# A two-layer transformer trunk in split fp32: transposes of x moved ahead of a gain transpose, one scaling ahead of a weight cast, and the MLP norms' squares ten steps later

## The chip, the cores and the metric

The kernel runs on one core of a Trainium2 chip. The metric is the device time of one execution in microseconds (us); lower is better. Unless a sentence says otherwise, a time within an execution counts from the start of the profiled span.

## The reference

x is a block of 256 tokens by 2048 columns. Two layers follow one another: the first mixes the tokens by softmax attention with a forget gate (FoX, 16 heads of 128), the second by attention in three dilated windows. Each mixer has an RMS norm ahead of it and an MLP with an RMS norm behind it, and everything adds into x. All is fp32.

```python
def rms_norm(x, g):
    xf = x.astype(jnp.float32)
    y = xf * lax.rsqrt(jnp.mean(xf * xf, axis=-1, keepdims=True) + EPS)
    return (y * g.astype(jnp.float32)).astype(x.dtype)

def sq_relu_mlp(h, w_up, w_down):
    a = jax.nn.relu(h @ w_up)
    return (a * a) @ w_down
...
    for i in range(DEPTH):
        j = i // N_MIXERS
        h = rms_norm(x, mix_norm_g[i])
        ...
        x = x + mix.astype(x.dtype)
        h = rms_norm(x, mlp_norm_g[i])
        x = x + sq_relu_mlp(h, mlp_w_up[i], mlp_w_down[i]).astype(x.dtype)
```

## The kernel before

**Weights.** The products stream the weights: 539 MB go through the DMA queues in one execution. A weight *unit* is 256 rows by 512 columns. Its transfer fills a tile `raw` (ring of 5); ScalarE rounds it to `wh` (L398, a cast to the reduced format that TensorE multiplies at full rate); VectorE takes the remainder `wl = raw - wh` (L399); both lie in rings of 5. The left operand exists in two parts likewise, so a product is three matmuls: `wh` with the high part (L447), `wl` with the high part (L448), `wh` with the low part (L449). A unit feeds 12 matmuls of 128x512. In the trace a unit has its number in the names: `raw141`, `wh141`, `wl141`. In some parts of the MLP's up projection a scheme with fewer products of combined operands is used (the "wide" tiles, L1138 to L1140); for it VectorE also forms `sd` and `v` out of two raw tiles (L395 to L402) and sums of the left operand (`sums`, below).

**Norms.** `norm_chain` (L609) runs once for each column block n of x (four blocks `x0` to `x3` of 512 columns). A norm's scale for each token, `rstd`, is applied behind the product, so the left operand needs only x transposed and multiplied by the gain: `hT`, eight pieces pr = 0 to 7, high and low part. For the first norm (`n0`) TensorE transposes x (L626, tiles `ptx`), ScalarE scales the result into the high part (L628) and VectorE makes the low part (L629). For the two MLP norms, `n1` (layer 1) and `n3` (layer 2), x is transposed by VectorE and by transfers (`transposed_by_dma`, tile `turned`); ScalarE scales it into `room` (L552) and casts it to `hT` (L555), VectorE makes the low part (L557). Behind that, `token_sums` adds the rooms (L592 to L594, VectorE), ScalarE casts the sums (L606), VectorE takes their remainder (L609).

Last in each chain ScalarE squares the block and sums along the row: two instructions for a block, one for each 128 tokens (L638, out to a scratch tile `junk`). When all four blocks are done, VectorE makes the mean (L645, L646, tile `ms`), GpSimd raises it to the power -1/2 (L647) and VectorE squares that (L649, `rstd2`). For n1 and n3 `rstd2` is first used by `add_chain`, behind the first down projection.

**Order.** The program is written as generators that a small scheduler (`jobs`) advances by one step, a *tick*, for each six matmuls: `yield 2` means "go on two steps later", `yield ("n1", 3)` means "when that is done". What is issued in a tick goes behind what was issued before it in each engine's queue, and a later pass keeps that order. So `yield later` in `norm_chain`, just ahead of the squares, sets behind which casts the squares stand on ScalarE. The function `later` comes with the call of `normed`; where none is given, it is 2 steps.

**The opening.** x0 comes in three transfers (128, 128 and 256 columns), with the gain rows (`mix_rows`) between the first two; then come weights and x1, x2, x3 in turn. `gain_columns("g_mix", ...)` transposes the gain rows on TensorE (L194, `ps_g_mix`) and VectorE copies them to `gain` (L195); each scaling reads `gain`. The first two units are cast in two halves (`split_part`).

Of the kernel before, what the change touches and what calls it, by code (L numbers as in the profile page):

```python
# [9 lines left out]
F32 = mybir.dt.float32  # L10
# [7 lines left out]
P = 128  # L18
D = 2048
S = 256  # L20
# [3 lines left out]
KC = D // P  # L24
# [95 lines left out]
def trunk(ctx: ExitStack, tc, x, fox_w_in, fox_b_f, fox_q_gain, fox_k_gain, fox_w_out, dil_w_in,  # L120
          dil_q_gain, dil_k_gain, dil_w_out, mix_norm_g, mlp_norm_g, mlp_w_up, mlp_w_down, out):
    nc = tc.nc
# [40 lines left out]
    ident = const.tile([P, P], F32, name="ident")  # L163
# [17 lines left out]
    MLP_G, FOX_G, DIL_G = 2 * KC + 8, 2 * KC, 2 * KC + 2  # L181

    def gain_rows(name, sources):
        rows = work.tile([2 * KC + 8, P], F32, tag="s", name=name, bufs=S_BUFS)
        at = 0
        for src in sources:
            nc.sync.dma_start(rows[at:at + src.shape[0], :], src)
            at += src.shape[0]
        return rows[0:at, :]

    def gain_columns(name, rows, at):
        n = rows.shape[0]
        ps = ps_tp.tile([P, 512], F32, tag="tp", name=f"ps_{name}")
        nc.tensor.transpose(ps[:, :n], rows, ident[:n, :n])  # L194
        nc.vector.tensor_copy(gain[:, at:at + n], ps[:, :n])  # L195
# [4 lines left out]
    xt = [act.tile([P, NT, NC], F32, tag=f"x{n}", name=f"x{n}") for n in range(NX)]  # L200
# [176 lines left out]
    def split(parts=(slice(0, W_SUB),)):  # L377
        i = state["split"]
        if i >= len(units):
            return  # L380
        hi = wpool.tile([P, W_SUB, NC], F32R, tag="wh", name=f"wh{i}", bufs=W_BUFS)
        lo = wpool.tile([P, W_SUB, NC], F32R, tag="wl", name=f"wl{i}", bufs=W_BUFS)
        splits.append((hi, lo))
        state["split"] += 1
        for part in parts:
            split_part(i, part)
        if parts:
            next_load()

    def split_part(i, part):  # L390
        n, of = units[i]
        raw, (hi, lo) = raws[n], splits[i]
        if of == "crossed":
            quarters[:] = [work.tile([P, RAW_SUB, NC], F32, tag=x, name=f"{x}_{n}", bufs=1) for x in ("sd", "v")]
            nc.vector.tensor_sub(quarters[0], raw, raws[n - 1][:, 1, :].unsqueeze(1).to_broadcast([P, RAW_SUB, NC]))  # L395
        elif of != "rows":
            raw = quarters[("differences", "sums").index(of)]
        nc.scalar.copy(hi[:, part, :], raw[:, part, :])  # L398
        nc.vector.tensor_sub(lo[:, part, :], raw[:, part, :], hi[:, part, :].bitcast(F32))  # L399
        if of == "crossed":  # L400
            nc.vector.tensor_add(quarters[1][:, 0, :], raw[:, 0, :], quarters[0][:, 1, :])
            nc.vector.tensor_sub(quarters[1][:, 1, :], raws[n - 1][:, 0, :], quarters[1][:, 0, :])  # L402
# [3 lines left out]
    def next_load():  # L406


        n, of = units[state["split"] - 1]
        spent.update({"rows": (n,), "crossed": (n - 1, n)}.get(of, ()))  # L410
        while state["done"] in spent:
            state["done"] += 1
        while state["raw"] < min(len(plan), state["done"] + RAW_BUFS):
            load()
# [98 lines left out]
    def norm_begin(tag):  # L513
        rstd[tag] = small.tile([P, NT], F32, tag="rstd", name=f"rstd_{tag}", bufs=2)
        hT[tag] = [None] * (KC // 2)
        return small.tile([P, NT, NX], F32, tag="ssp", name=f"ssp_{tag}", bufs=2)
# [97 lines left out]
    def norm_chain(tag, col, n, ssp, wait, later):  # L614
        yield wait
        if tag != "n0":
            yield from transposed_by_dma(tag, col, n)
        else:
            for half in range(2):
                pr = n * 2 + half  # L620
                both = act.tile([P, 2, 2, S], F32R, tag="hT", name=f"hT_{tag}_{pr}", bufs=KC // 2)
                for i, (pool, of) in enumerate(((ps_tp, "tp"), (ps_sc, "sc"))):
                    pt = pool.tile([P, S], F32, tag=of, name=f"ptx_{tag}_{pr}_{i}")
                    c = (half * 2 + i) * P
                    for t in range(NT):
                        nc.tensor.transpose(pt[:, t * P:(t + 1) * P], xt[n][:, t, c:c + P], ident)  # L626
                    gc = gain[:, col + pr * 2 + i:col + pr * 2 + i + 1]
                    nc.scalar.activation(both[:, i, 0, :], pt, AF.Copy, scale=gc)  # L628
                    nc.vector.scalar_tensor_tensor(both[:, i, 1, :], pt, gc, both[:, i, 0, :].bitcast(F32),  # L629
                                                   ALU.mult, ALU.subtract)  # L630
                hT[tag][pr] = both
                jobs.done.add((tag, pr))
                yield 1 if n < 2 else 2
        yield later
        for t in range(NT):
            junk = work.tile([P, NC], F32, tag="vw" if tag in ("n0", "n2") else "w", name=f"junk_{tag}_{n}_{t}",
                             bufs=1 if tag in ("n0", "n2") else 6)
            nc.scalar.activation(junk, xt[n][:, t, :], AF.Square, accum_out=ssp[:, t, n:n + 1])  # L638
        jobs.done.add((tag, "n", n))
        if n == NX - 1:  # L640
            for m in range(NX):
                yield (tag, "n", m)
            ms = small.tile([P, NT], F32, tag="ms", name=f"ms_{tag}", bufs=2)
            rstd[tag, 2] = small.tile([P, NT], F32, tag="rstd2", name=f"rstd2_{tag}", bufs=2)
            nc.vector.tensor_reduce(ms, ssp, AX.X, ALU.add)  # L645
            nc.vector.tensor_scalar(ms, ms, 1.0 / D, EPS, ALU.mult, ALU.add)  # L646
            nc.gpsimd.tensor_tensor(rstd[tag], ms, mhalf[:, :NT], ALU.pow)  # L647
            yield 2 if tag in ("n1", "n3") else 0
            nc.vector.tensor_mul(rstd[tag, 2], rstd[tag], rstd[tag])  # L649
            jobs.done.add((tag, "rstd"))  # L650
# [547 lines left out]
    def normed(tag, col, wait=lambda n: 2, later=lambda n: 2):  # L1198
        ssp = norm_begin(tag)
        return lambda n: norm_chain(tag, col, n, ssp, wait(n), later(n))  # L1200
# [10 lines left out]
    def load_x(n, lo=0, hi=NC):  # L1211
        hold(xt[n])
        nc.sync.dma_start(xt[n][:, :, lo:hi], xv[:, :, n * NC + lo:n * NC + hi])

    load_x(0, 0, P)
    mix_rows = gain_rows("g_mix", [mix_norm_g.rearrange(per_chunk, p=P)])
# [7 lines left out]
    for what in (lambda: load_x(1), load, load, lambda: load_x(2), load):  # L1224
        what()

    gain_columns("g_mix", mix_rows, 0)
    row_blocks = [slice(i, i + 1) for i in range(W_SUB)]
    split(())
    split_part(0, row_blocks[0])  # L1230
# [1 line left out]
    split_part(0, row_blocks[1])  # L1232
    next_load()
    split(())
    split_part(1, row_blocks[0])
    load_x(3)
    del issued["paced"]
    issued["opening"] = True

    def opening():  # L1240
        yield 1
        split_part(1, row_blocks[1])
        next_load()
        yield 2
        split(row_blocks)
        yield 1
        split()
        for _ in range(5):
            yield 2
            split()  # L1250
        yield 1
        del issued["opening"]
        while state["split"] - used[0] < W_BUFS:
            yield 4
            split()

    for n in range(1, NX):
        jobs.spawn(first(n))
    jobs.spawn(opening())
    jobs.spawn(more_constants())  # L1260


    tag = "n0"
    for j in range(4):
# [10 lines left out]
        for hh in range(4):  # L1275
# [2 lines left out]

    out_proj(lambda n: lambda k: ("of", k),
             lambda k: (oT["f", k // 4][0][:, k % 4, :], oT["f", k // 4][1][:, k % 4, :]),  # L1280
             normed("n1", MLP_G), group=3)
    jobs.spawn(dilation_tables())
    mlp("n1", then=normed("n2", KC))
    dilated("n2")
    out_proj(lambda n: lambda k: ("od", k // 2),
             lambda k: (oT["d", k // 4][0][:, k % 4, :], oT["d", k // 4][1][:, k % 4, :]),
             normed("n3", MLP_G + KC), group=3)
    mlp("n3", ready=store)
    while jobs.live:
        jobs.tick()  # L1290
# [29 lines left out]
```

## Time and profile before

| | |
|---|---|
| median of 3 runs | 2084.84 us (2084.24 to 2085.33) |
| the profiled execution: its own time | 2084.9 us |
| the profiled execution: its span | 2083.2 us |
| busy: TensorE (PE), its weight loads (PEld) | 2076.8 us (100%), 1818.5 us (87%) |
| busy: VectorE (DVE), ScalarE (ACT), GpSimd (POOL) | 1714.9 us (82%), 1305.8 us (63%), 275.2 us (13%) |
| granted TensorE clock | 9 in tenths in all 40 slices of the span |
| DMA | mean 259 GB/s |

Rows of the timeline view read: start in us, duration in us, engine, line, operation, output tile <- input tiles, sizes, count; in brackets, where there is one, the idle time ahead of it and what ended it. Matmuls overlap: a 128x512 matmul has a record of 0.38 us, but the next one starts 0.215 us behind it. Tile numbers are left out of the names, so a weight unit is told by its place. A line number belongs to the kernel before; behind the changed lines those of the kernel after are three to four higher.

### The profile page before, as it was taken

What the parts mean: (1) busy time and instruction counts of PE and PEld (TensorE: products, weight loads), DVE (VectorE), ACT (ScalarE), POOL (GpSimd) and SP (SyncE); (2) the same over time, 40 slices, a digit from 0 to 9 for tenths busy, and PEclk for the clock granted to TensorE, in tenths of its full rate; (3) what the DMA queues carried; (4) which work ended last, traced back from release to release, by engine and by line L of the source; (5) the groups of instructions that cost most, each with busy time, mean ns of one, the idle gap of its engine ahead of it and who ended that gap; (6) DMA issues with size and microseconds to landing.
All of it is one profiled execution on the core that took longest, in us unless ns stands there. A gap on an engine that the chain in (4) does not pass through costs nothing.

```text
span 2083.2 us, 28968 instructions
## 1 busy us (share of the span) xinstructions
PE 2076.8 (100%) x9835; PEld 1818.5 (87%) x9835; DVE 1714.9 (82%) x2183; ACT 1305.8 (63%) x1825; POOL 275.2 (13%) x398
## 2 busy tenths in 40 slices
PE   9999999999999999999999999999999999999999
PEld 7888888888888888888888888888888888888888
DVE  6888876898989889888668787766998898899874
ACT  6665654866666667564656565556766676666662
POOL 2000000011212111120010010000113031212120
PEclk9999999999999999999999999999999999999999
DMA  7888887888988898897877876877889888898885
GB/s 254 259 259 260 262 248 212 267 285 262 268 281 269 262 296 269 267 291 247 279 242 229 250 239 210 260 212 237 262 272 272 278 276 265 276 287 276 265 280 165
DMA packets 357205, 539.04 MB, mean 259 GB/s; under 512 B 43752, under 2 KB 144448, under 8 KB 357056
## 3 DMA queue, kind: packets, MB, share of 16 engines
q1 hardware_dynamic: 334624, 507.41, 76.8%
q0 software_dynamic: 22016, 29.38, 6.2%
q8 instruction: 77, 1.26, 0.3%
q10 hardware_dynamic: 416, 0.39, 0.1%
q14 instruction: 72, 0.59, 0.1%
HBM read 484.09 MB, written 40.39 MB: 252 GB/s over the span
## 4 chain that ended last, share of the span: by engine, by line
PE 97%; ACT 1%; DMA 1%; DVE 1%; issue 0%; SPq 0%; ACTq 0%; DVEq 0%
PE acc L448 26%; PE acc L447 26%; PE acc L449 25%; PE wide_n_tp L1139 2%; PE wide_n_tp L1140 2%; PE wide_n_tp L1138 2%; PE wide_n_sc L1139 2%; PE wide_n_acc L1140 2%; PE wide_n_acc L1139 2%; PE wide_n_sc L1140 2%; PE wide_n_sc L1138 2%; PE wide_n_acc L1138 2%; PE sc_d L798 0%; DMA raw<-in_fox_w_in_dram 0%; ACT room_n L552 0%; ACT wh L398 0%
## 5 line engine op out<-in xcount | busy, mean ns | idle before, releaser
L399 DVE TENSOR_TENSOR wl<-raw,wh 128x1024 fp32r<-128x1024 f32 (+1 forms) x763 | 919.5, 1214 | 308.5 <-ACT wh L398 299.3
L398 ACT CAST wh<-raw 128x1024 fp32r<-128x1024 f32 (+1 forms) x763 | 787.2, 1046 | 505.5 <-PE acc L449 368.7
L447 PE MATMUL acc<-wh,hT_n 128*128 128x512 f32 x1280 | 486.7, 380 | 0.4 <-ACT hT_n L628 0.2
L448 PE MATMUL acc<-wl,hT_n 128*128 128x512 f32 x1280 | 485.6, 379 | 0.5 <-DVE wl L399 0.5
L449 PE MATMUL acc<-wh,hT_n 128*128 128x512 f32 x1280 | 485.4, 379 | 0.0
L449 PEld LDWEIGHTS acc<-wh,hT_n 128*128 128x128 f32 x1280 | 241.9, 189 | 34.8 <-DVE hT_n L629 0.4
L448 PEld LDWEIGHTS acc<-wl,hT_n 128*128 128x128 f32 x1280 | 242.1, 189 | 34.6 <-DVE wl L399 2.1
L447 PEld LDWEIGHTS acc<-wh,hT_n 128*128 128x128 f32 x1280 | 242.1, 189 | 34.3 <-ACT hT_n L628 1.2
L447 PE MATMUL acc<-wh,aTh_n1a 128*128 128x512 f32 x512 | 194.0, 379 | 0.0
L448 PE MATMUL acc<-wl,aTh_n1a 128*128 128x512 f32 x512 | 194.0, 379 | 0.0
L449 PE MATMUL acc<-wh,aTl_n1a 128*128 128x512 f32 x512 | 194.0, 379 | 0.0
L447 PE MATMUL acc<-wh,aTh_n3a 128*128 128x512 f32 x480 | 181.9, 379 | 0.0
L448 PE MATMUL acc<-wl,aTh_n3a 128*128 128x512 f32 x480 | 181.9, 379 | 0.0
L449 PE MATMUL acc<-wh,aTl_n3a 128*128 128x512 f32 x480 | 181.9, 379 | 0.0
L994 POOL DMA_DIRECT2D x<-y_n x96 | 84.7, 1331 | 479.9 <-ACT y_n L993 421.4
L398 ACT CAST wh<-sd 128x1024 fp32r<-128x1024 f32 x80 | 84.1, 1051 | 99.4 <-DVE sd L395 77.6
L398 ACT CAST wh<-v 128x1024 fp32r<-128x1024 f32 x80 | 84.1, 1051 | 54.3 <-PE acc L449 42.7
L448 PEld LDWEIGHTS acc<-wl,aTh_n1a 128*128 128x128 f32 x512 | 96.8, 189 | 13.8
L447 PEld LDWEIGHTS acc<-wh,aTh_n1a 128*128 128x128 f32 x512 | 96.8, 189 | 13.7
L449 PEld LDWEIGHTS acc<-wh,aTl_n1a 128*128 128x128 f32 x512 | 96.8, 189 | 13.7
L449 PEld LDWEIGHTS acc<-wh,aTl_n3a 128*128 128x128 f32 x480 | 90.7, 189 | 12.9
L447 PEld LDWEIGHTS acc<-wh,aTh_n3a 128*128 128x128 f32 x480 | 90.7, 189 | 12.9
(665 smaller groups left out, 3227.7 us busy)
## 6 DMA issues: line engine op xcount, KB each, us to landing
raw<-in_mlp_w_up_dram SPq DMA_DIRECT2D x296, 512.0 KB, 4.9
raw<-in_mlp_w_down_dram SPq DMA_DIRECT2D x256, 512.0 KB, 5.0
raw<-in_dil_w_in_dram SPq DMA_DIRECT2D x192, 256.0 KB, 3.6
raw<-in_fox_w_in_dram SPq DMA_DIRECT2D x94, 512.0 KB, 4.7
raw<-in_fox_w_out_dram SPq DMA_DIRECT2D x32, 512.0 KB, 4.9
raw<-in_dil_w_in_dram SPq DMA_DIRECT2D x32, 512.0 KB, 5.4
raw<-in_dil_w_out_dram SPq DMA_DIRECT2D x32, 512.0 KB, 4.4
x<-y_n POOLq DMA_DIRECT2D x96, 128.0 KB, 6.4
```

The lines of the kernel that those rows point to most:

```text
L398: nc.scalar.copy(hi[:, part, :], raw[:, part, :])
L399: nc.vector.tensor_sub(lo[:, part, :], raw[:, part, :], hi[:, part, :].bitcast(F32))
L447: nc.tensor.matmul(acc[t], ah[:, tok], hi, start=first, stop=False)
L448: nc.tensor.matmul(acc[t], ah[:, tok], lo, start=False, stop=False)
L449: nc.tensor.matmul(acc[t], al[:, tok], hi, start=False, stop=last)
L994: nc.gpsimd.dma_start(xt[n][:, t, h * HC:h * HC + HC], y, accum_op=ALU.add)
L1138: nc.tensor.matmul(banks[bank], ah, wh, start=what < 3 and of == 0, stop=False, **alone)
L1139: nc.tensor.matmul(banks[bank], ah, wl, start=False, stop=False, **alone)
L1140: nc.tensor.matmul(banks[bank], al, wh, start=False, stop=of == KC // 2 - 1, **alone)
```

## The change

Three edits. First, in the n0 chain both transposes of a piece stand ahead of its two scalings, and for the first piece the gain rows' transpose and copy stand between the transposes and the scalings, instead of ahead of everything. Second, the first half of unit 1 is cast one tick into `opening()`, instead of ahead of the tick loop. Third, the chains of n1 and n3 wait twelve ticks ahead of the squares instead of two.

```diff
--- before.py
+++ after.py
@@ -619,11 +619,15 @@
             for half in range(2):
                 pr = n * 2 + half
                 both = act.tile([P, 2, 2, S], F32R, tag="hT", name=f"hT_{tag}_{pr}", bufs=KC // 2)
+                turned = []
                 for i, (pool, of) in enumerate(((ps_tp, "tp"), (ps_sc, "sc"))):
-                    pt = pool.tile([P, S], F32, tag=of, name=f"ptx_{tag}_{pr}_{i}")
+                    turned.append(pool.tile([P, S], F32, tag=of, name=f"ptx_{tag}_{pr}_{i}"))
                     c = (half * 2 + i) * P
                     for t in range(NT):
-                        nc.tensor.transpose(pt[:, t * P:(t + 1) * P], xt[n][:, t, c:c + P], ident)
+                        nc.tensor.transpose(turned[i][:, t * P:(t + 1) * P], xt[n][:, t, c:c + P], ident)
+                if pr == 0:
+                    gain_columns("g_mix", mix_rows, 0)
+                for i, pt in enumerate(turned):
                     gc = gain[:, col + pr * 2 + i:col + pr * 2 + i + 1]
                     nc.scalar.activation(both[:, i, 0, :], pt, AF.Copy, scale=gc)
                     nc.vector.scalar_tensor_tensor(both[:, i, 1, :], pt, gc, both[:, i, 0, :].bitcast(F32),
@@ -1224,7 +1228,6 @@
     for what in (lambda: load_x(1), load, load, lambda: load_x(2), load):
         what()
 
-    gain_columns("g_mix", mix_rows, 0)
     row_blocks = [slice(i, i + 1) for i in range(W_SUB)]
     split(())
     split_part(0, row_blocks[0])
@@ -1232,13 +1235,13 @@
     split_part(0, row_blocks[1])
     next_load()
     split(())
-    split_part(1, row_blocks[0])
     load_x(3)
     del issued["paced"]
     issued["opening"] = True
 
     def opening():
         yield 1
+        split_part(1, row_blocks[0])
         split_part(1, row_blocks[1])
         next_load()
         yield 2
@@ -1278,13 +1281,13 @@
 
     out_proj(lambda n: lambda k: ("of", k),
              lambda k: (oT["f", k // 4][0][:, k % 4, :], oT["f", k // 4][1][:, k % 4, :]),
-             normed("n1", MLP_G), group=3)
+             normed("n1", MLP_G, later=lambda n: 12), group=3)
     jobs.spawn(dilation_tables())
     mlp("n1", then=normed("n2", KC))
     dilated("n2")
     out_proj(lambda n: lambda k: ("od", k // 2),
              lambda k: (oT["d", k // 4][0][:, k % 4, :], oT["d", k // 4][1][:, k % 4, :]),
-             normed("n3", MLP_G + KC), group=3)
+             normed("n3", MLP_G + KC, later=lambda n: 12), group=3)
     mlp("n3", ready=store)
     while jobs.live:
         jobs.tick()
```

No instruction is added or taken away, and the orders of SyncE and GpSimd are as before. On TensorE only `ps_g_mix` moves, behind the first four transposes. Three places show the rest.

VectorE at the program's start (wl0 and wl1 are the remainders of units 0 and 1; hT_n0_0 and hT_n0_1 are the first two pieces of the left operand; the number at the end of a name only tells tiles apart). Before:

```order
L195 COPY gain_100<-ps_g_mix_136 128x32
L399 TENSOR_TENSOR wl0_140<-raw0_111,wh0_139 128x512
L629 SCALAR_TENSOR_TENSOR hT_n0_0_143<-ptx_n0_0_0_144,gain_100,hT_n0_0_143 128x256
L629 SCALAR_TENSOR_TENSOR hT_n0_0_143<-ptx_n0_0_1_149,gain_100,hT_n0_0_143 128x256
L399 TENSOR_TENSOR wl0_140<-raw0_111,wh0_139 128x512
L399 TENSOR_TENSOR wl1_160<-raw1_120,wh1_159 128x512
L629 SCALAR_TENSOR_TENSOR hT_n0_1_183<-ptx_n0_1_0_184,gain_100,hT_n0_1_183 128x256
L629 SCALAR_TENSOR_TENSOR hT_n0_1_183<-ptx_n0_1_1_189,gain_100,hT_n0_1_183 128x256
L399 TENSOR_TENSOR wl1_160<-raw1_120,wh1_159 128x512
```

After:

```order
L399 TENSOR_TENSOR wl0_137<-raw0_111,wh0_136 128x512
L195 COPY gain_100<-ps_g_mix_147 128x32
L633 SCALAR_TENSOR_TENSOR hT_n0_0_140<-ptx_n0_0_0_141,gain_100,hT_n0_0_140 128x256
L633 SCALAR_TENSOR_TENSOR hT_n0_0_140<-ptx_n0_0_1_144,gain_100,hT_n0_0_140 128x256
L399 TENSOR_TENSOR wl0_137<-raw0_111,wh0_136 128x512
L633 SCALAR_TENSOR_TENSOR hT_n0_1_181<-ptx_n0_1_0_182,gain_100,hT_n0_1_181 128x256
L633 SCALAR_TENSOR_TENSOR hT_n0_1_181<-ptx_n0_1_1_185,gain_100,hT_n0_1_181 128x256
L399 TENSOR_TENSOR wl1_160<-raw1_120,wh1_159 128x512 x2
```

The copy of the gain moves behind the first remainder, and the first half of unit 1's remainder moves behind piece 1's scaling; ScalarE's cast of that half and its scaling of piece 1 change places in the same way.

ScalarE in the middle of n1, at the casts of units 134 to 139 (junk_n1_0 are the squares of x0, junk_n1_1 of x1, and so on; sums_n1_0 are the sums of piece 0). Before:

```order
L398 CAST wh134_3887<-raw134_3706 128x1024
L606 CAST sums_n1_0_0_3893<-room_n1_0_0_3715 128x256
L606 CAST sums_n1_0_0_3893<-room_n1_0_1_3716 128x256
L638 ACTIVATE junk_n1_2_0_3903,ssp_n1_2960<-x2_103 128x512
L638 ACTIVATE junk_n1_2_1_3905,ssp_n1_2960<-x2_103 128x512
L398 CAST wh135_3917<-raw135_3735 128x1024
L398 CAST wh136_3938<-raw136_3764 128x1024
L606 CAST sums_n1_1_0_3944<-room_n1_1_0_3738 128x256
L606 CAST sums_n1_1_0_3944<-room_n1_1_1_3739 128x256
L398 CAST wh137_3962<-raw137_3797 128x1024
```

After:

```order
L398 CAST wh136_3926<-raw136_3764 128x1024
L606 CAST sums_n1_1_0_3932<-room_n1_1_0_3738 128x256
L606 CAST sums_n1_1_0_3932<-room_n1_1_1_3739 128x256
L642 ACTIVATE junk_n1_0_0_3942,ssp_n1_2960<-x0_101 128x512
L642 ACTIVATE junk_n1_0_1_3944,ssp_n1_2960<-x0_101 128x512
L398 CAST wh137_3954<-raw137_3793 128x1024
L398 CAST wh138_3975<-raw138_3838 128x1024
L606 CAST sums_n1_2_0_3981<-room_n1_2_0_3773 128x256
L606 CAST sums_n1_2_0_3981<-room_n1_2_1_3774 128x256
L642 ACTIVATE junk_n1_1_0_3993,ssp_n1_2960<-x1_102 128x512
L642 ACTIVATE junk_n1_1_1_3995,ssp_n1_2960<-x1_102 128x512
L398 CAST wh139_4005<-raw139_3883 128x1024
```

Before, x2's squares stand ahead of the cast of unit 135 (x0's stand further up, behind the cast of unit 131, and x1's just ahead of unit 134's). After, x0's stand ahead of the cast of unit 137 and x1's ahead of unit 139's; x2's follow ahead of unit 140's, and x3's move from behind unit 142's to behind unit 147's. In n3 the units with numbers higher by 476 stand in the same order.

VectorE behind the squares of n1 (ms_n1 is the mean, rstd2_n1 the scale squared). Before:

```order
L399 TENSOR_TENSOR wl141_4077<-raw141_3942,wh141_4076 128x1024
L399 TENSOR_TENSOR wl142_4095<-raw142_3966,wh142_4094 128x1024
L645 TENSOR_REDUCE ms_n1_4104<-ssp_n1_2960 128x2
L646 TENSOR_SCALAR ms_n1_4104<-ms_n1_4104 128x2
L399 TENSOR_TENSOR wl143_4122<-raw143_3987,wh143_4121 128x1024
L649 TENSOR_TENSOR rstd2_n1_4105<-rstd_n1_2959 128x2
```

After:

```order
L399 TENSOR_TENSOR wl147_4205<-raw147_4098,wh147_4204 128x1024
L649 TENSOR_REDUCE ms_n1_4214<-ssp_n1_2960 128x2
L650 TENSOR_SCALAR ms_n1_4214<-ms_n1_4214 128x2
L1060 STREAM_TRANSPOSE turned_n1a0_0_0_4225<-a_n1a0_0_0_4186 128x4x4x32
L399 TENSOR_TENSOR wl148_4235<-v_145_4136,wh148_4234 128x1024
L653 TENSOR_TENSOR rstd2_n1_4215<-rstd_n1_2959 128x2
```

The three small operations move from between units 142 and 144 to behind unit 147.

## The prediction

> **What bounds the kernel now.** I read the page first, then TensorE's timeline for its stalls, then ScalarE's and VectorE's timelines at those places.
>
> ```profile
> span 2083.2 us, 28968 instructions
> PE 2076.8 (100%) x9835; PEld 1818.5 (87%) x9835; DVE 1714.9 (82%) x2183; ACT 1305.8 (63%) x1825; POOL 275.2 (13%) x398
> PE 97%; ACT 1%; DMA 1%; DVE 1%; issue 0%; SPq 0%; ACTq 0%; DVEq 0%
> ```
>
> TensorE (PE) is the bound. It is busy 2076.8 of 2083.2 us, and 97% of the chain that ended last is its own. The change takes no matmul away, so all that there can be to gain is some of the 6.4 us in which PE does nothing, plus what its restarts cost; to lose there is whatever makes a weight unit late. The profiled execution took 2084.9 us, which the median of the runs (2084.84) equals within 0.1 us; so I add to 2084.9. About 0.2%, 4.2 us, is what a measurement of this kernel can tell from no change.
>
> The stalls at issue lie in n1, where the third edit works:
>
> ```profile
> 371.13 0.48 PE L447 MATMUL acc<-wh,hT_n 128*128 128x512 f32 x1
> 373.87 0.48 PE L447 MATMUL acc<-wh,hT_n 128*128 128x512 f32 x1
> ...
> 381.77 0.38 PE L447 MATMUL acc<-wh,hT_n 128*128 128x512 f32 x1
> 382.48 0.48 PE L448 MATMUL acc<-wl,hT_n 128*128 128x512 f32 x1 [0.33 <-DVE wl L399]
> 382.80 0.38 PE L449 MATMUL acc<-wh,hT_n 128*128 128x512 f32 x1
> ...
> 384.96 0.38 PE L447 MATMUL acc<-wh,hT_n 128*128 128x512 f32 x1
> 385.53 0.48 PE L448 MATMUL acc<-wl,hT_n 128*128 128x512 f32 x1 [0.18 <-DVE wl L399]
> ...
> 402.00:424.00 22.00, 22.00 (x103) 19.26 (x103) 21.51 (x32) 16.12 (x24) 6.15 (x11) 1.00 0.85 268
> ```
>
> The last row, of the view by windows (PE, PEld, DVE, ACT, POOL busy, clock, DMA), has 103 matmuls in 22.00 us without a stall: they follow each other every 0.215 us or a little less. One that had to wait has a record of 0.48 in place of 0.38, and its follower starts 0.32 behind it (382.48 to 382.80): a restart costs 0.10. The first two rows lose only that. The third starts 0.71 behind its forerunner and the fourth 0.57, so they lose 0.71 - 0.215 + 0.10 = 0.60 and 0.57 - 0.215 + 0.10 = 0.46. Together n1 loses 0.10 + 0.10 + 0.60 + 0.46 = 1.26 us.
>
> **The change part by part.**
>
> *The squares leave their old places.* ScalarE (ACT) in n1:
>
> ```profile
> 367.34 1.04 ACT L398 CAST wh<-raw 128x1024 fp32r<-128x1024 f32 x1 [1.70 <-DMA raw<-in_mlp_w_up_dram]
> 368.29 0.63 ACT L638 ACTIVATE junk_n<-x 128x512 f32<-128x512 f32 x1
> ...
> 369.53 1.26 ACT L552 ACTIVATE room_n<-turned_n,gain 128x128 f32<-128x128 f32 x4
> ...
> 386.49 0.71 ACT L606 CAST sums_n<-room_n 128x256 fp32r<-128x256 f32 x2 [1.33 <-DVE room_n L594]
> 387.11 1.99 ACT L398 CAST wh<-raw 128x1024 fp32r<-128x1024 f32 x2
> ...
> 391.04 1.99 ACT L398 CAST wh<-raw 128x1024 fp32r<-128x1024 f32 x2
> ```
>
> The cast at 367.34 is unit 131's. It waited for a transfer, so it starts there in any order, and everything below counts from it. x0's pair of squares behind it takes 369.53 - 368.29 = 1.24 us, and the scaling into `room` waits for it. Without it hT's pieces 2 and 3, for which PE stopped at 371.13 and 373.87, come 1.24 earlier, and so do unit 134's remainder (382.48) and, with x2's pair gone too, unit 135's (385.53). All four stalls are shorter than 1.24, so they go: -1.26 us.
>
> *The squares arrive in their new places.* VectorE (DVE) beside it:
>
> ```profile
> 381.21 1.22 DVE L399 TENSOR_TENSOR wl<-raw,wh 128x1024 fp32r<-128x1024 f32 x1
> 384.25 1.23 DVE L399 TENSOR_TENSOR wl<-raw,wh 128x1024 fp32r<-128x1024 f32 x1 [1.15 <-ACT wh L398]
> ...
> 388.18 1.23 DVE L399 TENSOR_TENSOR wl<-raw,wh 128x1024 fp32r<-128x1024 f32 x1
> ...
> 392.11 1.22 DVE L399 TENSOR_TENSOR wl<-raw,wh 128x1024 fp32r<-128x1024 f32 x1
> ...
> 398.28 1.22 DVE L399 TENSOR_TENSOR wl<-raw,wh 128x1024 fp32r<-128x1024 f32 x1
> ```
>
> From 386.49 ACT and DVE take turns: ACT casts sums, then unit 137 (387.11, two casts in 1.99, so the first ends at about 388.1); DVE starts on it at 388.18, adds the next rooms, and ACT, idle for 1.33, takes them up. The next round stands at 391.04 and 392.11. There is no slack in the cast at the head of a round, so x0's pair ahead of unit 137's cast and x1's ahead of unit 139's delay the loop by 1.24 each; x2's, ahead of unit 140's cast, is followed by rooms, hT casts and the cast of unit 141 on ACT without a gap, and delays these by 1.24. Added: 3 x 1.24 = 3.72 up to unit 141's remainder (398.28). Taken away ahead of it: x0's pair and x2's (DVE at 384.25 had waited 1.15 for ACT). x1's pair stood ahead of unit 134's cast, but DVE came to that unit at 381.21 without idle, so that pair had been free. Unit 141's remainder is late by 3.72 - 2.48 = 1.24.
>
> ```profile
> 401.17 0.38 PE L448 MATMUL acc<-wl,hT_n 128*128 128x512 f32 x1
> ...
> 425.77 0.38 PE L448 MATMUL acc<-wl,hT_n 128*128 128x512 f32 x1
> ```
>
> PE uses it at 401.17. It is done at 398.28 + 1.22 = 399.50, and a start behind a remainder comes 0.05 later (384.25 + 1.23 = 385.48, 385.53): 1.62 to spare. That is eaten by 1.24 of lateness and by PE's own 1.26, since without its stalls it comes earlier: 1.24 + 1.26 - 1.62 = 0.88 of new stall and 0.10 of restart, 0.98 us given back at one place.
>
> *The rest of n1.* The next units without room are those in the wide part:
>
> ```profile
> 401.30 1.23 DVE L399 TENSOR_TENSOR wl<-raw,wh 128x1024 fp32r<-128x1024 f32 x1 [0.40 <-ACT wh L398]
> 423.75 1.18 DVE L399 TENSOR_TENSOR wl<-raw,wh 128x1024 fp32r<-128x1024 f32 x1
> ```
>
> x3's pair no longer stands ahead of the cast for which DVE waits 0.40 at 401.30, and the two small mean operations (between the end of two remainders, 398.28 + 2 x 1.17, and 401.30 - 0.40, so 0.3) leave that place: DVE's 1.24 shrink to about 0.55. But the operations return behind unit 147 (+0.3, rstd2 a little more), and from 402 to 424 DVE is busy 21.51 of 22.00 us (the row by windows above), so it recovers hardly anything: I take 0.9 at unit 153 (423.75), between 0.4, if all that idle is used, and 1.24. That unit had 425.77 - 424.93 - 0.05 = 0.79 to spare; PE is still 1.26 - 0.98 = 0.28 early. So 0.9 + 0.28 - 0.79 = 0.39, and with two restarts, since unit 152 just ahead is about as tight, 0.59. n1 in all: -1.26 + 0.98 + 0.59 = +0.3 us. With 0.4 in place of 0.9 nothing is lost here, and n1 comes to -0.3; with 1.24, to +0.65.
>
> *n3.* The same order, other slack:
>
> ```profile
> 1441.66 1.04 ACT L398 CAST wh<-raw 128x1024 fp32r<-128x1024 f32 x1 [0.68 <-DMA raw<-in_mlp_w_up_dram]
> ...
> 1459.51 0.38 PE L447 MATMUL acc<-wh,hT_n 128*128 128x512 f32 x1
> 1459.85 0.48 PE L448 MATMUL acc<-wl,hT_n 128*128 128x512 f32 x1
> ...
> 1472.62 1.22 DVE L399 TENSOR_TENSOR wl<-raw,wh 128x1024 fp32r<-128x1024 f32 x1
> 1475.49 0.38 PE L448 MATMUL acc<-wl,hT_n 128*128 128x512 f32 x1
> ...
> 1498.10 1.19 DVE L399 TENSOR_TENSOR wl<-raw,wh 128x1024 fp32r<-128x1024 f32 x1
> 1500.10 0.38 PE L448 MATMUL acc<-wl,hT_n 128*128 128x512 f32 x1
> ```
>
> Here PE has one stall to lose: 0.34 - 0.215 + 0.10 = 0.23. And transfers lead the casts (1441.66 waits for one), so taking x0's pair from behind it lets the next cast run into its own transfer; of 1.24 between 0 and all is gained, and I take 0.4, near the lower end, because of that row. Unit 617 (1472.62, 141's counterpart) is late by 3.72 - 1.24 - 0.4 = 2.08 (bounds 1.24 and 2.48). To spare it had 1475.49 - 1473.84 - 0.05 = 1.60: a stall of 2.08 + 0.23 - 1.60 = 0.71, with restart 0.81. At unit 629 (1498.10) DVE is late by 2.08 - 0.35 = 1.73 as in n1, spare 1500.10 - 1499.29 - 0.05 = 0.76, PE by now 0.58 late itself: 1.73 - 0.76 - 0.58 = 0.39, with restarts 0.59. n3: -0.23 + 0.81 + 0.59 = +1.17 us (+0.2 to +1.6 with 1.24 and 2.48 put through the same steps).
>
> *The opening.*
>
> ```profile
> 5.14 0.28 PE L194 MATMUL ps_g_mix<-ident,g_mix 32*128 32x32 f32 x1 [0.26 <-POOL x L360]
> 5.35 1.11 PE L626 MATMUL ptx_n<-ident,x 128*128 128x128 f32 x4
> 6.60 0.48 PE L447 MATMUL acc<-wh,hT_n 128*128 128x512 f32 x1
> ...
> 6.57 0.77 SPq L1213 DMA_DIRECT2D x<-in_x_dram  x1
> ...
> x<-in_x_dram SPq DMA_DIRECT2D x1, 512.0 KB, 9.2
> 15.44 0.38 PE L449 MATMUL acc<-wh,hT_n 128*128 128x512 f32 x1
> 15.86 0.63 PE L626 MATMUL ptx_n<-ident,x 128*128 128x128 f32 x4
> ```
>
> The gain's transpose now stands behind four transposes, which take 1.11 with their tail, so the copy of `gain` and with it the first scaling come later: by 0.2 to 0.7, I estimate 0.35 (the transposes can start some 0.2 earlier, since they need not wait for the gain rows). Piece 1's scaling, ahead of the cast now, comes earlier, and unit 1's first remainder later. But PE cannot pass 15.86: these are x2's first transposes, and x2's transfer is issued at 6.57 and takes 9.2, to 15.8. The matmul ahead, at 15.44, makes room at 15.65 already, so PE has 0.2 of waiting there; 0.35 of delay overshoots by some 0.1 at most. So no gain is possible here, and I put +0.05 (0 to +0.35).
>
> *Other parts.* `rstd2` comes some ten ticks later, but is first read behind the first down projection, hundreds of us on. GpSimd's power operation and its transfers keep their order.
>
> **Sum.** 0.31 + 1.17 + 0.05 = +1.5: 2084.9 + 1.5 = 2086.4 us. The bounds add up to -0.1 and +2.6: 2084.8 to 2087.5.
>
> **The rivals.**
>
> *A, nothing is given back* (0.18): the loop of 386 to 398 has more slack than its rows show, say because sums can wait. Then the stalls only go: -1.26 - 0.23 = -1.5, 2083.4 us. For it: PE waits for none of the sums there. Against it: the cast at 387.11 and the remainder at 388.18 touch.
>
> *B, gain and loss cancel* (0.12): the stall at unit 141 comes as worked out, but n3's lateness is at its lower bound, so that unit 617 just arrives in time (1.24 + 0.23 - 1.60 is below 0), and DVE recovers in the wide part: -1.26 + 0.98 - 0.23 = -0.5, 2084.4 us. For it: DVE's 0.40 of idle at 401.30. Against it: the 21.51 of 22 us that it is busy behind that.
>
> *C, slower by over 0.2%* (0.05): the squares' removal is not passed on, because DVE's queue and not ACT's leads up to 386, while the added 3.72 are. Then the four stalls stay, units 141 and 617 stall by 3.72 - 1.62 + 0.10 = 2.2 and 3.72 - 1.60 + 0.10 = 2.2, and the wide part adds 0.59 twice: +5.6, 2090.5 us. It decides from a lateness of about 3 us at both units. Against it: 384.25's wait of 1.15 for ACT.
>
> *D, the clock opens later* (0.04): the four transposes at 5.35 take 1.11, the same four at 15.86 only 0.63, so PE runs slower until about the first product. The change leaves PE without work between its transposes and a first product at about 6.95. If that holds the clock down as long again, to about 13 us, some 15 matmuls at half rate cost 0.215 each, up to 3.2 us on top of the forecast, 2089.6; half of that gives 2088.0. Against it: PE had waited before, 0.26 at 5.14, and ran fast soon after all the same.
>
> The page of the Trainium skill "TensorE: Matmul & The Clock Gate" (Part 1, "What's actually happening") speaks against the change here: the clock is full only after a busy window of some 3.4 us, which runs freely, so that the moment varies from run to run. By the page, one window more would cost an estimated 1.7 us, half its length; the two transposes' rows agree with a slow start, and no row here shows what an idle gap does to it.
>
> **How the numbers follow.** The forecast, give-back larger than gain, has 0.61; A has 0.18, B 0.12, D 0.04, C 0.05. The range reaches from A's time, with 0.1 for its spread, over B and the forecast's bounds to D's middle with a little for stalls that I have not found: 2083.3 to 2088.2. Faster by over 0.2% would need 4.2 of 6.4 idle us: 0.02. Slower by over 0.2%, beyond 2089.0, is C and the upper part of D: 0.06. The rest, 0.92, lies within.
>
> **What would show it.** Right: no idle at 371 to 386, a new wait of PE for `wl` of 0.7 to 1 us near 400.8 and one of 0.6 to 0.8 near 1476, and smaller ones near 424 and 1499; first product at about 6.95, x2's transposes at 15.9. Wrong: no wait of PE for `wl` near 401 (A), stalls left at 382 and 385 (C), or x2's transposes later than 16.2.

## The result and the profile after

The change makes the kernel slower by about a sixth of a per cent: 2087.89 us (median of 20 runs, 2085.64 to 2089.37) against 2084.12 (20 runs, 2083.22 to 2085.77). The ratio of the mean times is 1.0017, with a 95% interval of 1.001 to 1.0024; the ratios below are of means too, so they can differ a little from what the medians give. That is +3.8 us where +1.5 was forecast. The time lies inside the range (2083.3 to 2088.2), near its upper end.

The page of the kernel after, its first lines, and what TensorE (PE) waited for (total us, times, longest):

```profile
span 2086.5 us, 28961 instructions
PE 2078.4 (100%) x9835; PEld 1819.6 (87%) x9835; DVE 1715.4 (82%) x2183; ACT 1305.0 (63%) x1825; POOL 274.5 (13%) x398
...
PE 91%; DVE 4%; ACT 2%; DMA 1%; issue 1%; SPq 0%; DVEq 0%; ACTq 0%
```

```profile
PE acc L448 <- DVE wl L399: 1.9, 5, 0.9
PE acc L447 <- ACT hT_n L632: 0.8, 1, 0.8
```

The profiled execution took 2088.6 us, 3.7 more than that of before, and its span is 3.3 longer. PE's own share of the chain that ended last has fallen from 97% to 91%. The two waits above are new in size: 0.8 ahead of the first product, and five for weight remainders, one of them (0.24) in the opening and the other four at the places shown further down.

PE's timeline in the opening:

```profile
5.05 1.40 PE L627 MATMUL ptx_n<-ident,x 128*128 128x128 f32 x4 [0.16 <-POOL x L360]
6.37 0.31 PE L194 MATMUL ps_g_mix<-ident,g_mix 32*128 32x32 f32 x1
7.48 0.79 PE L447 MATMUL acc<-wh,hT_n 128*128 128x512 f32 x1 [0.79 <-ACT hT_n L632]
8.07 0.63 PE L448 MATMUL acc<-wl,hT_n 128*128 128x512 f32 x1
8.49 0.63 PE L449 MATMUL acc<-wh,hT_n 128*128 128x512 f32 x1
...
17.80 0.60 PE L627 MATMUL ptx_n<-ident,x 128*128 128x128 f32 x4
```

The first product starts at 7.48 (6.60 before), and the first six product matmuls have records of 0.63 or more and follow each other every 0.43 us instead of 0.215. x2's first transposes come at 17.80 (15.86 before): 1.94 us lost up to there.

The places of n1 and n3 that the prediction named:

```profile
373.04 0.38 PE L447 MATMUL acc<-wh,hT_n 128*128 128x512 f32 x1
...
383.61 0.38 PE L448 MATMUL acc<-wl,hT_n 128*128 128x512 f32 x1
...
402.90 0.48 PE L448 MATMUL acc<-wl,hT_n 128*128 128x512 f32 x1 [0.86 <-DVE wl L399]
...
428.01 0.48 PE L448 MATMUL acc<-wl,hT_n 128*128 128x512 f32 x1 [0.17 <-DVE wl L399]
...
1478.21 0.48 PE L448 MATMUL acc<-wl,hT_n 128*128 128x512 f32 x1 [0.44 <-DVE wl L399]
...
1503.32 0.48 PE L448 MATMUL acc<-wl,hT_n 128*128 128x512 f32 x1 [0.17 <-DVE wl L399]
```

The records of 0.48 at 371 to 386 have become 0.38, so the four stalls of n1 are gone. In their place PE stops for units 141 (402.90), 153 (428.01), 617 (1478.21) and 629 (1503.32): the four that the prediction named.

Why unit 141 is late shows on ScalarE (ACT) and VectorE (DVE). The last two rows are of the view by windows, the upper one of the kernel before, all other rows of the kernel after:

```profile
387.41 0.61 ACT L642 ACTIVATE junk_n<-x 128x512 f32<-128x512 f32 x1
...
388.02 1.98 ACT L398 CAST wh<-raw 128x1024 fp32r<-128x1024 f32 x2
389.08 1.23 DVE L399 TENSOR_TENSOR wl<-raw,wh 128x1024 fp32r<-128x1024 f32 x1 [1.14 <-ACT wh L398]
...
386.00:402.00 16.00, 16.00 (x76) 14.01 (x75) 14.60 (x27) 14.18 (x30) 0.70 (x1) 1.00 0.80 267
386.00:402.00 16.00, 16.00 (x74) 13.59 (x72) 11.69 (x23) 14.51 (x36) 0.00 (x0) 1.00 0.79 260
```

The cast of unit 137 waits behind x0's squares (the row at 387.41 is the second of the pair), and DVE, which in the kernel before went on to this unit without a pause, now idles 1.14 for it. Between 386 and 402 DVE is busy 11.69 of 16 us, where it was busy 14.60 before.

### The profile page after: what moved, and what is told of

It is laid out like the page before. It is cut to its first block, busy times and chain, and to the rows that moved or that the text cites. A ratio compares the mean times of both kernels' runs of the same rounds, so it can differ in the third digit from the quotient of the medians.

```text
span 2086.5 us, 28961 instructions
## 1 busy us (share of the span) xinstructions
PE 2078.4 (100%) x9835; PEld 1819.6 (87%) x9835; DVE 1715.4 (82%) x2183; ACT 1305.0 (63%) x1825; POOL 274.5 (13%) x398
## 3 DMA queue, kind: packets, MB, share of 16 engines
q8 instruction: 77, 1.26, 0.3%
## 4 chain that ended last, share of the span: by engine, by line
PE 91%; DVE 4%; ACT 2%; DMA 1%; issue 1%; SPq 0%; DVEq 0%; ACTq 0%
PE acc L448 24%; PE acc L447 24%; PE acc L449 24%; PE wide_n_tp L1143 2%; PE wide_n_tp L1144 2%; PE wide_n_tp L1142 2%; DVE wl L399 2%; PE wide_n_acc L1143 2%; PE wide_n_acc L1144 2%; PE wide_n_acc L1142 2%; PE wide_n_sc L1143 2%; PE wide_n_sc L1144 2%; PE wide_n_sc L1142 2%; ACT room_n L552 1%; DMA turned_n<-blocks_n 1%
```

## The experiments

All are edits of the kernel before unless the text says otherwise, timed in alternation with it on the same chip. There were three sessions, each on another chip: late_only, open_only, gain_first and open_filled, with a median of before of 2083.8 us; late60, x0_only, before_again and after_again (2084.13); open60, open60_filled, late60_wake8 and late_only_b (2084.67). So times of different sessions are compared by their distance from before. The versions whose names end in `_again` or `_b` ran once. To compare the profiled executions I add up, for each, by how much every product matmul starts later than in the execution that has it earliest, relative to its forerunner; the table gives this for the stretches of n1 (360 to 395, and 395 to 440 of the kernel before) and of n3, less what late60, which has no stall there, shows. "Slow first" is the number of product matmuls at the pitch of 0.43.

| kernel | time of the profiled execution | slow first | x2's transposes at | 360-395 | 395-440 | n3 |
|---|---|---|---|---|---|---|
| before | 2084.9 | 0 | 15.86 | 1.34 | 0.00 | 0.23 |
| before_again | 2085.25 | 0 | 16.13 | 0.70 | 0.05 | 0.14 |
| after | 2088.6 | 6 | 17.80 | 0 | 1.78 | 1.22 |
| after_again | 2087.73 | 6 | 17.66 | 0 | 1.02 | 1.23 |
| late_only | 2087.26 | 7 | 17.09 | 0 | 1.30 | 0.74 |
| late_only_b | 2085.79 | 0 | 15.25 | 0 | 1.71 | 1.01 |
| open_only | 2085.66 | 6 | 17.49 | 0.68 | 0 | 0 |
| gain_first | 2085.33 | 7 | 17.02 | 0.84 | 0 | 0 |
| open_filled | 2084.22 | 0 | 16.11 | 0.68 | 0 | 0 |
| x0_only | 2084.15 | 0 | 15.27 | 0.37 | 0.57 | 0 |
| late60 | 2084.39 | 7 | 16.95 | 0 | 0 | 0 |
| open60 | 2083.43 | 0 | 15.97 | 0 | 0 | 0 |
| open60_filled | 2085.01 | 6 | 17.54 | 0 | 0 | 0 |
| late60_wake8 | 2084.52 | 8 | 17.06 | 0 | 0 | 0 |

By the same sums the executions agree behind the opening and outside these columns within 0.15 us, but for 0.6 in before_again and 0.3 in late_only near 90 us, a place that no edit touches.

**late_only: the third edit alone.**

```diff
-             normed("n1", MLP_G), group=3)
+             normed("n1", MLP_G, later=lambda n: 12), group=3)
...
-             normed("n3", MLP_G + KC), group=3)
+             normed("n3", MLP_G + KC, later=lambda n: 12), group=3)
```

> The kernel before with only the third edit (squares of n1 and n3 twelve ticks later). Theory one (the clock opens later because of the opening's edits, and the squares cost what they cost in the profile after, +0.41 in n1 and +0.98 in n3): the opening is as before (first product at 6.6, x2's first transposes at 15.9), stalls near 401, 426, 1476, 1500 as after; +1.4 us over before. Rival (the squares cost it all, and the late opening was only this one execution's): +3.3 to +3.8 us.

Measured: 2087.2 against 2083.8 us, ratio 1.0016 (1.0007 to 1.0025), so +3.4: the rival's number. But its profile does not carry the rival: the stalls at 401 to 440 and in n3 add up to 2.0 us, and the opening, which it shares instruction for instruction with the kernel before, was slow here too:

```profile
6.92 0.80 PE L447 MATMUL acc<-wh,hT_n 128*128 128x512 f32 x1
7.51 0.63 PE L448 MATMUL acc<-wl,hT_n 128*128 128x512 f32 x1
7.93 0.63 PE L449 MATMUL acc<-wh,hT_n 128*128 128x512 f32 x1
```

So the slow pitch does not need the edits of the opening, and +3.4 of the +3.8 comes with the third edit alone.

**open_only: the opening's two edits alone** (the kernel after, with `later` taken out of both calls).

> The kernel after with the squares at their old place, so the opening's two edits alone. Theory one: the first six product matmuls follow each other at about 0.43 us as after, x2's first transposes stand near 17.8; +1.9 to +2.4 us over before, with the stalls of n1 at 371 to 386 back. Rival (the opening is hidden by x2's transfer, the late opening was only one execution's): +0.0 to +0.3 us.

Measured: 2084.71 against 2083.8, ratio 1.0005 (0.9996 to 1.0013): between the two. The profile has the slow pitch, as theory one wanted, and x2's transposes come 1.6 us later than in the profile of before, but the median is up by 0.9 only.

**gain_first: open_only with the gain rows first again.**

```diff
-                if pr == 0:
-                    gain_columns("g_mix", mix_rows, 0)
...
+    gain_columns("g_mix", mix_rows, 0)
     row_blocks = [slice(i, i + 1) for i in range(W_SUB)]
```

> The opening's edits without the move of the gain rows: ps_g_mix and its copy stand first again; the second scaling stays ahead of unit 1's first cast, squares at their old place. Theory one (what costs is the gap between the transposes and the first product, which the late gain makes): no gap, full pitch from the first product, 0.0 us (-0.2 to +0.3) against before. Rival (the scaling ahead of the cast costs, since unit 1's remainder comes late): about +1 us or more, with a wait for wl near 11.

Measured: 2085.21 against 2083.8, ratio 1.0003 (0.9994 to 1.0012). No gap in front of the first product (6.54), and still seven matmuls at the slow pitch: a miss for theory one. The rival's wait for wl near 11 isn't there either: in the first 30 us the profile shows waits of PE only for the zeros of the spare matmuls and, 0.2 us, ahead of `ps_g_mix`. The eleven times fall into two groups, 2083.3 to 2084.1 (five) and 2085.2 to 2086.0 (six), so the median says little.

**open_filled: open_only with the gap filled.**

```diff
                 if pr == 0:
                     gain_columns("g_mix", mix_rows, 0)
+                    wake(2)
```

> As open_only, with two more spare matmuls right behind ps_g_mix, which fill the gap in front of the first product (0.79 us of idle after). Theory one in its form that the idle gap keeps the clock down: the first products run at the full pitch of 0.215, and of the opening's +1.9 to +2.4 at least 1.2 goes. Rival (the gap only shifts the work, and the clock opens by the time since start): the products run at 0.43 until about 10 us as in open_only, and nothing goes.

Measured: 2084.95 against 2083.8, ratio 1.0005 (0.9996 to 1.0014). The profiled execution ran at the full pitch from the first product, as theory one said, but the times are those of open_only. One execution is no test of it; open60 and open60_filled below are.

**late60: the squares sixty ticks later instead of two.**

```diff
+             normed("n1", MLP_G, later=lambda n: 60), group=3)
...
+             normed("n3", MLP_G + KC, later=lambda n: 60), group=3)
```

> The kernel before with the squares of n1 and n3 sixty ticks later instead of two: they stand behind the casts of units 164 to 178 on ScalarE (where that engine waits for matmuls, 451.70 to 478.90 in the profile before) and not in the loop of 386 to 398. Theory one (squares cost only where ScalarE's casts have no slack): no stall at 401, 426, 1476 and 1500, and the stalls at 371 to 386 gone or smaller; -0.5 to -1.5 us against before. Rival (squares that come late cost by themselves, by the ring they write to or by the late scale): +1 us or more, as late_only's +3.4.

Measured: 2083.93 against 2084.13, ratio 0.9997 (0.9988 to 1.0006). In the profile PE waits for no weight and no hT at all behind the first spare matmul; ACT, where the squares now stand, still waits for PE next to them:

```profile
PE spare L175 <- DVE zeros L171: 1.5, 1, 1.5
PE ps_g_mix L194 <- DMA g_mix<-in_mix_norm_g_dram: 0.4, 1, 0.4
```

```profile
450.38 0.61 ACT L638 ACTIVATE junk_n<-x 128x512 f32<-128x512 f32 x1
...
451.39 1.05 ACT L398 CAST wh<-raw 128x1024 fp32r<-128x1024 f32 x1 [0.31 <-PE acc L449]
```

So being late shows no cost of its own; the rival's +1 us or more lies at the edge of the interval (-2.5 to +1.3 us), and no wait in the profile speaks for it. With the old opening twelve ticks stand at +3.4 against before and sixty at -0.2.

**x0_only: x0's squares alone at twelve.**

```diff
+             normed("n1", MLP_G, later=lambda n: 12 if n == 0 else 2), group=3)
...
+             normed("n3", MLP_G + KC, later=lambda n: 12 if n == 0 else 2), group=3)
```

> The kernel before with only x0's squares of n1 and n3 twelve ticks later; those of x1, x2, x3 stay at two. Theory one: one pair in the loop instead of three, so unit 141 is no later than before (+1.24 - 1.24) and has 1.6 of room less the 0.6 to 1.3 by which PE comes earlier: no stall at 401, hardly any at 426; -0.3 to -1.2 us against before. Rival (each pair in the loop costs a third of late_only's +3.4): +1 us.

Measured: 2084.74 against 2084.13, ratio 1.0004 (0.9995 to 1.0013). No stall at 401, as theory one has it for one pair in the loop, none in n3, and what was left at 360 to 395 fell to 0.37; but unit 153 made PE wait, which had been expected to be hardly anything:

```profile
424.64 0.48 PE L448 MATMUL acc<-wl,hT_n 128*128 128x512 f32 x1 [0.17 <-DVE wl L399]
```

So 0.57 of what PE gained ahead is lost again in the wide part, where DVE is busy 21.51 of 22.00 us in the kernel before. The time, +0.6 us, misses theory one's -0.3 to -1.2 and is nearer to the rival's +1; of this, 0.4 lies outside the span (see below).

**before_again and after_again: both kernels unchanged, for a second profile.**

> The kernel before once more, unchanged, for a second profile. Theory one (the clock's opening and the landing of unit 131 vary between executions, and the first profile had an early opening and a late landing): the matmuls from 6.6 on at either pitch, 0.215 or 0.43, unit 131 waits for its transfer between 0.4 and 1.7 us, and n1's stalls together are between 0.5 and 1.3 us. Rival (the first profile is what before always does): pitch 0.215 and 1.26 us again within 0.1.

> The kernel after once more, unchanged, for a second profile. Theory one: pitch 0.43 of the first products, as the gap at 6.7 to 7.5 is there in each execution; stalls near 401, 426, 1476 and 1500 with 1.0 to 2.2 us together. Rival (the slow pitch is a matter of chance alone): either pitch.

Measured: the second execution of before lost 0.70 in n1 at 360 to 395, not 1.34 (1.26 by the rows of the prediction), with unit 131's wait for its transfer at 1.20, not 1.70. The first profile had shown more to gain than is usual: in open_only, gain_first and open_filled, where the squares stand as before, it was 0.68 to 0.84. The second execution of after has the slow pitch again and stalls at the same four units, 2.25 us together (3.0 in the first).

**open60 and open60_filled: the opening of after, with the squares at sixty; the second with `wake(2)` as in open_filled.**

> The opening's two edits with the squares sixty ticks later, so that n1 and n3 have no stall to hide or add anything and the spread of the times shows the opening alone. late60, with the opening of before, fell into two groups, spans 2081.0 to 2081.6 (5 runs) and 2082.2 to 2083.1 (6 runs), and its profiled run, of the upper group, had the slow pitch of 0.43 in the first seven product matmuls. Theory one (the gap of 0.8 us in front of the first product keeps the clock down in nearly every execution): most of the runs above a span of 2082.5. Rival (the slow pitch is chance in either opening, the edits only delay the first product): two groups again, each 0.2 to 0.6 above late60's, about half and half.

> open60 with two spare matmuls behind ps_g_mix, which fill the gap. Theory one: most runs in a lower group, spans about 2081.2 to 2082.0. Rival: the same two groups as open60, about half and half.

Measured: open60 2083.6, ratio 0.9997 (0.9989 to 1.0006); open60_filled 2084.98, ratio 1.0 (0.9992 to 1.0009); before 2084.67. Eight of open60's eleven runs have spans of 2081.5 to 2082.1, and its profiled execution ran at the full pitch behind the very gap:

```profile
5.99 0.25 PE L194 MATMUL ps_g_mix<-ident,g_mix 32*128 32x32 f32 x1
7.03 0.48 PE L447 MATMUL acc<-wh,hT_n 128*128 128x512 f32 x1 [0.79 <-ACT hT_n L632]
7.35 0.38 PE L448 MATMUL acc<-wl,hT_n 128*128 128x512 f32 x1
```

open60_filled, without the gap, did not:

```profile
6.35 1.22 PE L175 MATMUL spare<-zeros 128*128 128x512 f32 x2
7.37 0.64 PE L447 MATMUL acc<-wh,hT_n 128*128 128x512 f32 x1
7.80 0.63 PE L448 MATMUL acc<-wl,hT_n 128*128 128x512 f32 x1
```

My theory that the gap keeps the clock down in nearly every execution falls. Whether it shifts the odds can't be told from so few profiles: behind the gap of about 0.8 us the pitch was slow in three of four, without it in five of ten.

The times show no cost of the opening's edits: open60 is not slower than before. The table does show one when like is compared with like. Among the profiles at the slow pitch, x2's first transposes stand at 16.95 to 17.09 where the gain rows come first (late60, late60_wake8, late_only, gain_first) and at 17.49 to 17.80 where they come behind x's transposes (open_only, after, after_again, open60_filled). As gain_first shares all but the gain's move with open_only, it is this move that costs there, between profiles of one chip 0.4 to 0.7 us. At the full pitch (15.25 to 16.13 against 15.97 and 16.11) nothing can be told.

**late60_wake8: late60 with one spare matmul more.**

```diff
-    wake(7)
+    wake(8)
```

> late60 with eight spare matmuls at the start instead of seven, which closes the 0.26 us of idle ahead of ps_g_mix. If work without a gap opens the clock sooner, more runs than late60's 5 of 11 lie in the lower group, and the median is 0.3 to 1.2 us under late60's; if chance decides, it is as late60 within 0.6.

Measured: 2082.93 against 2084.67, ratio 0.9994 (0.9985 to 1.0003), the lowest median of all. Seven of eleven runs have spans up to 2081.6, against late60's five: the direction that was hoped for, but on another chip and no more than chance can do, and the interval holds 1. It is not shown that any version beats the kernel before.

**late_only_b: late_only once more.**

> late_only again for a second profile. If its +3.4 holds without a slow opening, the pitch of the first products is 0.215 and the stall at 401 is larger than the 0.8 of its first profile; if the slow opening is a part of it in most executions, the pitch is 0.43 again.

Measured: 2085.79, full pitch from 6.34 on and x2's transposes at 15.25, and a larger stall in n1:

```profile
6.34 0.48 PE L447 MATMUL acc<-wh,hT_n 128*128 128x512 f32 x1 [0.34 <-ACT hT_n L628]
6.66 0.38 PE L448 MATMUL acc<-wl,hT_n 128*128 128x512 f32 x1
...
400.30 0.48 PE L448 MATMUL acc<-wl,hT_n 128*128 128x512 f32 x1 [0.86 <-DVE wl L399]
```

One program, two executions: slow pitch and 2087.26, full pitch and 2085.79. They ran on different chips, but each of the three chips showed both pitches among its kernels. So the pitch of the opening differs between executions of one kernel without any edit. That it does so on one chip is likely, not shown.

## Why the prediction was right, point by point

**The time is inside the range partly by luck.** The median of 2087.89 lies above the forecast's own bounds (2084.8 to 2087.5); it is inside only because the range was stretched to rival D's middle for a chance of 0.04. And the sum started from 2084.9, which the longer series of before puts 0.8 too high (2084.12). Counted from before, the range ends at +3.3 and the change cost +3.8. One of the prediction's own signs of being wrong came too: x2's transposes stand at 17.80, later than 16.2. A slip in the bounds changes nothing: with both restarts, n3's lower bound comes to +0.33, not +0.2.

**The squares leave their old places: right in kind, too large.** All four stalls went. But the term, -1.26 us, was read from one execution, in which n1's stalls were about twice their usual size: 0.70 in the second profile of before, 0.68 to 0.84 in the three kernels that left the squares alone. Together with n3's 0.23 (0.14 the second time) the usual gain is 0.7 to 0.9, not 1.5.

**The squares arrive in their new places: right in place and kind, near in size.** Forecast 0.98 for unit 141, 0.59 for the wide part, 0.81 and 0.59 in n3, 2.97 in all; the profile after has 1.78 + 1.22 = 3.0, and the three others with all squares at twelve 2.25, 2.0 and 2.7. So that the first profile met 2.97 almost exactly is luck: unit 141 cost 0.5 to 1.3 in these four and unit 617 0.2 to 0.7, while the wide part stayed at about 0.5 each time. The argument by the loop (three pairs between a cast and its remainder, none of which can hide) is supported by x0_only, where one pair makes no stall at 401, and by late60, where none is left.

**The opening: the term +0.05 failed in the profiled executions.** The first lost 1.94 us there, 0.88 by the first product (forecast 0.35) and the rest by six matmuls at the slow pitch, 6 x 0.215 = 1.3, less what PE's waits for weights hid: what rival D had described. D's cause, the gap, is neither needed nor enough, though: the slow pitch came with the old opening too (late_only, late60, late60_wake8), and a full pitch came behind the gap (open60). At the full pitch the term can't be tested to 0.1: open60's x2 transposes stand at 15.97, within the 15.25 to 16.13 of the old opening. At the slow pitch it was too small: the gain's move costs 0.4 to 0.7 there. The bound "PE cannot pass 15.86" was also one execution's: 15.25 and 15.27 in late_only_b and x0_only.

The page of the Trainium skill "TensorE: Matmul & The Clock Gate" (Part 1, "What's actually happening") says that the moment of the clock's opening varies with a free-running window of some 3.4 us. These runs agree with this part: in fourteen profiled executions the product matmuls were slow for none (six executions) or for six to eight in a row (eight), up to 9.5 to 10.7 us, and one kernel had both. The spread of 500 ns either way that the same section gives for that moment is too small for them: late_only's first profile was slow until past 10.3 us, its second at the full pitch from 6.34.

**Rivals.** A (nothing given back) and C (old stalls stay) are out by the rows at 402.90 and 383.61. B's condition, DVE recovering in the wide part, didn't hold (428.01).

**What makes up +3.8.** Between the two profiled executions the rows account for all of it. The span is 3.3 longer: 1.94 in the opening (17.80 against 15.86), 0.44 in n1 (1.78 - 1.34) and 0.99 in n3 (1.22 - 0.23). Forecast were 0.05, 0.31 and 1.17. Another 0.4 lies outside the span, a term that the prediction did not have: time less span is 2.0 to 2.2 us in every run of after, late_only and x0_only (2088.6 - 2086.5, 2084.15 - 2082.1), and 1.7 to 1.8 in those of all others; the profile does not show what it is. So in this pair the squares came out as forecast, and the miss is the opening and the 0.4.

The medians say something else, and it isn't settled. The third edit alone has +3.4. Its give-back of 2.0 to 2.7 less the usual gain of 0.7 to 0.9, with the 0.4 outside the span, makes +1.5 to +2.4; 1.0 to 1.9 stay open. A slow pitch in most runs of late_only would fit: it costs x2's transposes 0.8 to 1.8 us in the old opening, and nine of late_only's eleven spans are 2084.7 or more, nearer to its slow profile (2085.2) than to its full one (2083.7). But the pitch of a run without a profile isn't on record, and pitch alone does not sort the times: both profiles of before had the full pitch and took 2084.9 and 2085.25, more than its median. Why late_only, with the old opening, should be slow more often than before, no run shows.

## What to carry to other kernels

An instruction that nobody waits for still delays all that is queued behind it, so it belongs where its engine waits for the bound engine, not just "later": twelve steps put three pairs of squares into a loop of two engines without slack, sixty put them where no cost shows. A stall that one profile shows is a sample; before it enters a sum as a gain, a second profile of the same kernel tells whether it is usually that large. The same holds for the time that a sum starts from. Give-backs can be forecast from rows of "ready" and "used": 2.97 us here, where four executions showed 2.0 to 3.0.

## What the runs showed of the hardware that was not expected

The view by windows gives the granted clock as 1.00 in the opening too (0 to 5 and 7.5 to 10.7 us of the kernel after), while the start-to-start times there are 0.43 us for the same matmul that later takes 0.215; the pitch has to be read from the matmuls' own rows. And kernels that differ only in the order of a few instructions in the middle (before and late_only) differ by 0.4 us in what lies outside the span, in every one of their runs; the cause is open.
